# First weight units of the next block split before the meeting point, into tiles that are dead by then, and a third gate pair of layer one issued earlier

## The chip, the cores and the metric

The kernel runs on one core of a Trainium2 chip. Five engines take part, each with its own instruction queue: TensorE (PE; its weight loads are shown as PEld), VectorE (DVE), ScalarE (ACT), GpSimd (POOL) and SyncE (SP), which issues the DMAs. The metric is the device time of one execution in microseconds. Before the change the median of three runs is 835.58 us.

## The reference

The program computes a two-layer encoder on 256 tokens of width 1024 in float32. Each layer has a token mixer and a feed-forward network (FFN), each inside two normalisations:

```python
h = rmsnorm(x, g_mix_pre[l])
z = h @ w_in[l] + b_in[l]
y_m = mlstm_branch(...) @ w_up_mlstm[l]          # 4 heads of 128, both directions
y_f = fourier_branch(...) @ w_up_fourier[l]
y_s = s5_branch(...)                             # ends in a gated product with w_glu
gates = sigmoid(z[..., OFF_GATE:])               # three gates of width 1024
mixed = gates[0]*y_m + gates[1]*y_f + gates[2]*y_s
x = x + rmsnorm(mixed @ w_out[l], g_mix_post[l])
h = rmsnorm(x, g_ffn_pre[l])
f = square(relu(h @ w_ffn1[l])) @ w_ffn2[l]      # d_ff = 4096
x = x + rmsnorm(f, g_ffn_post[l])
```

So there are four blocks in a row (mixer 0, FFN 0, mixer 1, FFN 1), and the step from a block to the next is always the same: a sum over the whole width, a normalisation, the residual, another normalisation, and then the first product of the next block.

## The kernel before

**Weights.** All weights arrive in float32 and are multiplied in three products (high by high, high by low, low by high). A unit of weights is a tile of 128 x 1024 elements. `wload` makes one in three steps: a DMA on SP's queue into a `raw` tile (L200), ScalarE rounds it to the high part `whi` (L202), VectorE subtracts to get the low part `wlo` (L204). The `raw` tiles come from a ring of five, `whi` and `wlo` from rings of four; some units go to two larger rings, `ringA` and `ringB`, which other data use too. A slot of `raw` is free when `wlo` is done, one of `whi` and `wlo` when the last matmul of that unit is.

**Two forms of product.** In the body of a block the weights are the stationary operand and the tokens stream, 256 columns at a time (`mm3`, L262 to L264). At the start of a block the tokens are normalised one half (t=0, 128 tokens) after the other (t=1), and the first output columns are computed with the tokens stationary and the weights streaming, 512, 272 or 256 columns at a time (`tokens`, L278 to L281). In `tokens`, `hhi` and `hlo` are the high and low parts of the transposed normalised tokens, shown as `hT`. For t=0 the products with the low parts of the weights are put last (L295), for t=1 they stand beside the others.

**The meet.** Between two blocks `meet` puts together four strands: the last products of the old block for t=0 (`products(0)`) and t=1 (`products(1)`, "P"), the chains of normalisation for t=0 ("0") and t=1 ("1"), and the first units of the next block's weights, a `Feed` with the rounding of a unit ("h") and its subtraction ("l"). A chain runs through: two squares on ScalarE (L378), a small power on GpSimd (L340, L342), the gain and the residual on VectorE (L380, L386), two squares again (L355), GpSimd again, the second gain on VectorE (L361), eight transposes on TensorE (L188), and the high and low part of the result on ScalarE and VectorE (L370, L371). The string `MEET` gives the order of these steps on ScalarE and VectorE; the order on TensorE, and of what has no letter in the string, comes from a scheduler. Meet 0 is between mixer 0 and FFN 0, meet 1 between FFN 0 and mixer 1 (between the layers), meet 2 between mixer 1 and FFN 1.

**The Feed.** For an FFN it holds six units: four of 512 columns and two of 256. For layer 1's mixer it holds three units of the gates' projection of 272 columns (`igf`) and four of the values' projection `v`, 512 columns. `meet` empties it.

**The end of a mixer.** After the Fourier part, gates and products alternate: the mLSTM heads are normalised (L964), transposed and gated (L974) into `ym` (high part L976 on ScalarE, low part L977 on VectorE, both in `ringB`). `glu_up` multiplies the S5 result with `w_glu`, `own_gate` computes a gate for 256 output columns, and `mlstm_up` multiplies `ym` with `w_up_mlstm` and adds the gated parts. Two of the four own gates are issued before `glu_up`, two inside `mlstm_up`.

## Time and profile before

| | |
|---|---|
| median of three runs | 835.58 us (835.45 to 836.53) |
| the profiled execution | 834.29 us, of which the span from first to last instruction is 831.6 us |
| granted TensorE clock, mean | 0.998 of full speed |
| TensorE busy | 810.7 us of 831.6 (97%), 5825 matmuls |
| VectorE busy | 597.6 us (72%) |
| ScalarE busy | 472.4 us (57%) |
| GpSimd busy | 30.3 us (4%) |

The durations in a timeline are those of single instructions. Matmuls overlap each other, so for TensorE the distance from one start to the next is what an instruction costs, not its duration. "x8" joins eight instructions in a row, and the number in brackets is the idle time of the engine just before, with the instruction that ended it. Idle time of an engine other than TensorE costs nothing by itself.

### The profile page before, as it was taken

To read this page: it belongs to the slowest core of one execution; us is meant where nothing else is said; L and a number is where in the kernel's file an instruction comes from. 1 tells how busy PE (TensorE), PEld (TensorE's weight loads), DVE (VectorE), ACT (ScalarE), POOL (GpSimd) and SP (SyncE) were. 2 spreads that over 40 slices of the span, in tenths; PEclk is the share of its full clock that TensorE was granted. 3 is DMA by queue.
4 is the path that set the end of the run, shared out by engine and by line. 5 is a ranking of instruction groups with operands and counts; after the bars stand their busy time and mean duration, and the time that the engine had idled before them with its cause. 6 is when DMAs were issued, how large, how long until landed. Compare 5 with 4: busy or idle time off the path is not lost.

```text
span 831.6 us, 14910 instructions
## 1 busy us (share of the span) xinstructions
PE 810.7 (97%) x5825; PEld 749.4 (90%) x5825; DVE 597.6 (72%) x1071; ACT 472.4 (57%) x784; POOL 30.3 (4%) x51
## 2 busy tenths in 40 slices
PE   7999999998999999999999999999999999999996
PEld 5899999998878999999879999999997899999995
DVE  5898899887685567667568798776876755555563
ACT  4668764586464458467654355666865444444451
POOL 1000200000020000000010010000000100000000
PEclk9999999999999999999999999999999999999999
DMA  8785843554755564765837554555666555566651
GB/s 264 222 229 142 247 121 103 152 177 148 257 138 179 185 188 137 235 186 186 271 96 229 152 179 128 152 178 153 176 185 215 181 158 193 185 186 195 181 174 50
DMA packets 122262, 147.87 MB, mean 178 GB/s; under 512 B 22310, under 2 KB 104398, under 8 KB 121936
## 3 DMA queue, kind: packets, MB, share of 16 engines
q1 hardware_dynamic: 122044, 146.66, 57.9%
q8 instruction: 45, 0.74, 0.4%
q10 hardware_dynamic: 148, 0.27, 0.1%
q14 instruction: 25, 0.20, 0.1%
HBM read 144.33 MB, written 2.57 MB: 177 GB/s over the span
## 4 chain that ended last, share of the span: by engine, by line
PE 71%; DVE 2%; ACT 1%; issue 1%; POOL 1%; DVEq 0%; POOLq 0%; ACTq 0%
PE mm L262 12%; PE mm L264 12%; PE mm L263 12%; PE acc L263 8%; PE acc L264 8%; PE acc L262 8%; PE mm L279 2%; PE mm L278 2%; PE mm L295 1%; PE mm L188 1%; PE mm L281 1%; PE acc L743 1%; PE acc L939 1%; DVE wlo L204 1%; DVE x_sb L386 0%
## 5 line engine op out<-in xcount | busy, mean ns | idle before, releaser
L204 DVE TENSOR_TENSOR wlo<-raw,whi 128x1024 fp32r<-128x1024 f32 (+1 forms) x237 | 287.6, 1215 | 153.1 <-ACT whi L202 152.1
L202 ACT ACTIVATE whi<-raw 128x1024 fp32r<-128x1024 f32 (+1 forms) x237 | 248.5, 1052 | 241.3 <-PE mm L263 141.6
L262 PE MATMUL mm<-hT,whi 128*128 128x256 f32 x1024 | 290.9, 284 | 0.0
L264 PE MATMUL mm<-hT,wlo 128*128 128x256 f32 x1024 | 290.4, 284 | 0.0
L263 PE MATMUL mm<-hT,whi 128*128 128x256 f32 x1024 | 290.2, 283 | 0.0
L262 PEld LDWEIGHTS mm<-hT,whi 128*128 128x128 f32 x1024 | 192.8, 188 | 1.5
L263 PEld LDWEIGHTS mm<-hT,whi 128*128 128x128 f32 x1024 | 192.9, 188 | 1.1
L264 PEld LDWEIGHTS mm<-hT,wlo 128*128 128x128 f32 x1024 | 193.3, 189 | 0.2
L263 PE MATMUL acc<-wlo,ringB 128*128 128x512 f32 x280 | 109.3, 392 | 0.7 <-DVE wlo L204 0.7
L264 PE MATMUL acc<-whi,ringB 128*128 128x512 f32 x280 | 108.8, 391 | 0.0
L262 PE MATMUL acc<-whi,ringB 128*128 128x512 f32 x280 | 106.2, 390 | 0.0
L263 PEld LDWEIGHTS acc<-wlo,ringB 128*128 128x128 f32 x280 | 52.6, 188 | 12.1 <-DVE wlo L204 1.9
L264 PEld LDWEIGHTS acc<-whi,ringB 128*128 128x128 f32 x280 | 52.6, 188 | 11.0
L262 PEld LDWEIGHTS acc<-whi,ringB 128*128 128x128 f32 x280 | 52.6, 188 | 10.2
L279 PE MATMUL mm<-whi,hT 128*128 128x512 f32 (+1 forms) x84 | 30.3, 369 | 1.9 <-DVE hT L371 1.8
L906 DVE SCALAR_TENSOR_TENSOR t1k<-ringB,pc,t1k 128x254 f32<-128x254 f32 (+1 forms) x64 | 31.0, 484 | 0.9
L278 PE MATMUL mm<-whi,hT 128*128 128x512 f32 (+1 forms) x84 | 30.5, 373 | 0.7 <-ACT whi L202 0.5
L262 PE MATMUL mm<-ringB,whi 128*128 128x256 f32 x96 | 27.4, 286 | 1.7 <-ACT ringB L976 1.7
L380 DVE SCALAR_TENSOR_TENSOR w2k<-acc,ringA 128x512 f32<-128x512 f32 x16 | 10.6, 688 | 24.7 <-ACT t1k L378 24.7
L263 PE MATMUL mm<-ringB,whi 128*128 128x256 f32 x96 | 27.3, 285 | 0.0
L264 PE MATMUL mm<-ringB,wlo 128*128 128x256 f32 x96 | 27.2, 284 | 0.0
L378 ACT ACTIVATE t1k<-acc 128x512 bf16<-128x512 f32 x16 | 9.5, 595 | 30.4 <-PE acc L264 30.4
(334 smaller groups left out, 1156.8 us busy)
## 6 DMA issues: line engine op xcount, KB each, us to landing
raw<-in_w_ffn_dram SPq DMA_DIRECT2D x128, 512.0 KB
raw<-in_w_in_dram SPq DMA_DIRECT2D x84, 512.0 KB
raw<-in_w_out_dram SPq DMA_DIRECT2D x16, 512.0 KB
raw<-in_w_glu_dram SPq DMA_DIRECT2D x16, 256.0 KB
raw<-in_w_up_mlstm_dram SPq DMA_DIRECT2D x8, 512.0 KB
ringB<-md SPq DMA_DIRECT2D x2, 1024.0 KB
raw<-in_w_up_fourier_dram SPq DMA_DIRECT2D x4, 512.0 KB
raw<-in_w_in_dram SPq DMA_DIRECT2D x4, 408.0 KB
```

What stands on the lines that cost most here:

```text
L188: nc.tensor.transpose(o, i, cst[:k, C_ID:C_ID + k])
L202: act(hi, raw, AF.Copy)
L204: latest[0] = V.tensor_sub(lo, raw, hi.bitcast(F32)).ins
L262: mm(o, lhi, rhi, start=start, stop=False)
L263: mm(o, lhi, rlo, start=False, stop=False)
L264: mm(o, llo, rhi, start=False, stop=stop)
L278: mm(o, hhi[:, k, tt], hi, start=k == 0, stop=False)
L279: mm(o, hlo[:, k, tt], hi, start=False, stop=False)
L281: mm(o, hhi[:, k, tt], lo, start=False, stop=k == NK - 1)
L378: act(junk(), ps[c], AF.Square, accum_out=ss[:, c:c + 1])
L380: stt(f, ps[c], ROOT_D, gpost[:, half(c)], ALU.mult, ALU.mult)
L906: stt(u[:, lo_:hi_], z[:, lo_ + o:hi_ + o], col(l, "cw", j * 8 + i), u[:, lo_:hi_], ALU.mult, ALU.add)
```

## The change

Five things are changed together.

- The ring of `raw` tiles has four slots in place of five. The room goes to a small tile `pre`; the S5 tables `QT` and `Wt` become two tiles each for every layer, and `yg`, `oth` and `gx` are tiles that can be taken again under the same name once they are dead.
- `Feed` units get places: an FFN's four units of 512 columns go to `QT0`, `QT1`, `Wt0`, `Wt1`, the first of 256 columns to `tabC` and `tabS`, the last to the ring of `whi`. Layer 1's first two `igf` units go to `oth` with `yg` and to `gx` with `pre`.
- These units are split before the meet: after the second and fourth step of `glu_up` and after the first three of `mlstm_up` for the FFN's, in the FFN's steps 12 and 14 for layer 1's `igf`. The strings of `MEET` become shorter accordingly, and both layers use the same one.
- `tokens` issues four high products, then (for t=1) four with the low weights, then four with `hlo`, where it alternated one by one.
- In layer 0 three own gates are issued before `glu_up`, not two.

The diff, cut to its core:

```diff
-MEET = (("l0h0lh0l0Pl1hh1ll11ll", "hl0h0hlh0l0hPl1h1llll11l"), "hl0h0llP0101h11")
+MEET = ("0000Phl1111", "00P0hl0h1l1h1h1")
-    wp = ctx.enter_context(tc.tile_pool(name="wp", bufs=5))
+    wp = ctx.enter_context(tc.tile_pool(name="wp", bufs=4))
...
         raw = wp.tile(shape, F32, tag="raw", name=nm("raw"))
-        if in_ring:
+        if isinstance(in_ring, tuple):
+            if len(in_ring) == 1:
+                both = per([P, 2] + shape[1:], in_ring[0], F32R)
+                hi, lo = both[:, 0], both[:, 1]
+            else:
+                hi, lo = (per(shape, tag, F32R) for tag in in_ring)
+        elif in_ring:
...
-    def tokens(t, parts, together):
+    def tokens(t, parts, together, step=NK // 2):
...
-            for k in range(NK):
-                hi, lo = (w[:, k % kn, :] for w in units[k // kn])
-                mm(o, hhi[:, k, tt], hi, start=k == 0, stop=False)
-                mm(o, hlo[:, k, tt], hi, start=False, stop=False)
+            def part(a, i, ks, last=False):
+                for k in ks:
+                    mm(o, a[:, k, tt], units[k // kn][i][:, k % kn, :], start=k == 0 and a is hhi and i == 0,
+                       stop=last and k == NK - 1)
+
+            for k0 in range(0, NK, step):
+                ks = range(k0, min(k0 + step, NK))
+                part(hhi, 0, ks)
                 if t > 0:
-                    mm(o, hhi[:, k, tt], lo, start=False, stop=k == NK - 1)
+                    part(hhi, 1, ks)
+                part(hlo, 0, ks, t > 0)
...
-        return Feed([(iu, pieces_of(w, k0, min(3, NK - k0), OFF_IG, NIGF)) for k0 in (0, 3, 6)] +
+        spare = [None] * 3 if l == 0 else [("oth", "yg"), ("gx", "pre"), None]
+        return Feed([(iu, (*pieces_of(w, k0, min(3, NK - k0), OFF_IG, NIGF), spare[k0 // 3])) for k0 in (0, 3, 6)] +
...
                 stt(pair(th1, n2), z1, 0.5, pair(th1, n2), ALU.mult, ALU.add)
+                if n2 % 2:
+                    after.lo()
                 tick(B)
...
                 put_mix(mix, n2, th0)
+                if n2 < 3:
+                    after.lo()
 
         fourier_up()
-        gates = [own_gate(n2) for n2 in range(2)]
+        gates = [own_gate(n2) for n2 in range(3 if l == 0 else 2)]
...
-    GROUPS = ((512, None), (256, "A"))
+    GROUPS = ((512, [("QT0",), ("QT1",), ("Wt0",), ("Wt1",)]), (256, [("tabC", "tabS"), None]))
...
             f1(c)
+            if c >= NF // 2 - 4 and c % 2 == 0:
+                after.lo()
```

Where this moves instructions shows at two meets. The first place is ScalarE's queue in meet 1, from the steps that follow the transposes of t=0 (before: around them) to the second `v` unit, here `ringA_5088`. `acc` L378 and `x_sb` L355 are the two pairs of squares of t=1. Before:

```order
L378 ACTIVATE t1k_5050,ss_5049<-acc_3257 128x512
L378 ACTIVATE t1k_5054,ss_5049<-acc_3258 128x512
L370 ACTIVATE hT_84<-acc_5062 128x4x128
L370 ACTIVATE hT_84<-acc_5069 128x4x128
L355 ACTIVATE t1k_5079,ss_5078<-x_sb 128x512
L355 ACTIVATE t1k_5081,ss_5078<-x_sb 128x512
L202 ACTIVATE whi_5004<-raw_5003 128x1024
L370 ACTIVATE hT_84<-acc_5095 128x4x128
L370 ACTIVATE hT_84<-acc_5102 128x4x128
L202 ACTIVATE ringA_5088<-raw_5087 128x1024
```

The same place after the change, where L394, L371 and L386 are the former L378, L355 and L370, and `ringA_5069` is the second `v` unit:

```order
L386 ACTIVATE hT_5_84<-acc_5054 128x4x128
L386 ACTIVATE hT_5_84<-acc_5061 128x4x128
L213 ACTIVATE whi_4922<-raw_4921 128x1024
L394 ACTIVATE t1k_5073,ss_5072<-acc_3255 128x512
L394 ACTIVATE t1k_5077,ss_5072<-acc_3256 128x512
L371 ACTIVATE t1k_5089,ss_5088<-x_sb_78 128x512
L371 ACTIVATE t1k_5091,ss_5088<-x_sb_78 128x512
L213 ACTIVATE ringA_5069<-raw_5068 128x1024
L213 ACTIVATE ringA_5098<-raw_5097 128x1024
L213 ACTIVATE whi_5242<-raw_5241 128x1024
```

The squares of the sum (L394) have moved behind the high parts of t=0 and behind the first `v` unit `whi_4922`; the second `v` unit follows the squares of t=1 in both, and directly so now.

TensorE's queue at the same meet, before, from the last products of `igf` for t=0 to the transposes of t=1 (`acc_5095`, `acc_5102`); `mm_5155` are the values of t=0:

```order
L295 MATMUL mm_5129<-wlo_4969,hT_84 128x272 x3
L295 MATMUL mm_5129<-wlo_4988,hT_84 128x272 x2
L278 MATMUL mm_5155<-whi_5004,hT_84 128x512
L279 MATMUL mm_5155<-whi_5004,hT_85 128x512
L278 MATMUL mm_5155<-whi_5004,hT_84 128x512
L279 MATMUL mm_5155<-whi_5004,hT_85 128x512
L188 MATMUL acc_5095<-cst,w2k_5091 128x128 x4
L188 MATMUL acc_5102<-cst,w2k_5093 128x128 x4
```

After the change, with `mm_5162` as the values of t=0 and `acc_5109`, `acc_5116` as the transposes of t=1:

```order
L311 MATMUL mm_5136<-wlo_4801,hT_5_84 128x272 x2
L289 MATMUL mm_5162<-whi_4922,hT_5_84 128x512 x2
L289 MATMUL mm_5162<-ringA_5069,hT_5_84 128x512 x2
L289 MATMUL mm_5162<-whi_4922,hT_6_85 128x512 x2
L289 MATMUL mm_5162<-ringA_5069,hT_6_85 128x512 x2
L192 MATMUL acc_5109<-cst_79,w2k_5101 128x128 x4
L289 MATMUL mm_5162<-ringA_5098,hT_5_84 128x512 x2
L192 MATMUL acc_5116<-cst_79,w2k_5103 128x128 x4
```

Products with the second `v` unit, `ringA_5069`, stand now ahead of the transposes of t=1, and one pair with the third unit between them; before, only the first unit did.

The second place is VectorE's queue in meet 0, the chain of t=1 from its first gain (before L380) to its second (before L361). Before:

```order
L380 SCALAR_TENSOR_TENSOR w2k_3070<-acc_2902,ringA_2893 128x512
L380 SCALAR_TENSOR_TENSOR w2k_3074<-acc_2903,ringA_2893 128x512
L386 SCALAR_TENSOR_TENSOR x_sb<-w2k_3070,rs_480_3078,x_sb 128x512
L386 SCALAR_TENSOR_TENSOR x_sb<-w2k_3074,rs_480_3078,x_sb 128x512
L204 TENSOR_TENSOR ringA_3063<-raw_3062,ringA_3063 128x1024
L204 TENSOR_TENSOR ringA_3081<-raw_3080,ringA_3081 128x1024
L361 SCALAR_TENSOR_TENSOR w2k_3098<-x_sb,rs_487_3094,ringA_2893 128x512
L361 SCALAR_TENSOR_TENSOR w2k_3100<-x_sb,rs_487_3094,ringA_2893 128x512
```

After the change, where L396, L402, L215 and L377 are the former L380, L386, L204 and L361; the units 3260, 3290 and 3327 are later weights of the FFN, and ScalarE's queue has their three roundings between the two pairs of squares of t=1, where it had two of `ringA`:

```order
L396 SCALAR_TENSOR_TENSOR w2k_3075<-acc_2928,ringA_2923 128x512
L396 SCALAR_TENSOR_TENSOR w2k_3079<-acc_2929,ringA_2923 128x512
L402 SCALAR_TENSOR_TENSOR x_sb_78<-w2k_3075,rs_498_3083,x_sb_78 128x512
L215 TENSOR_TENSOR wlo_3260<-raw_3258,whi_3259 128x1024
L402 SCALAR_TENSOR_TENSOR x_sb_78<-w2k_3079,rs_498_3083,x_sb_78 128x512
L215 TENSOR_TENSOR wlo_3290<-raw_3288,whi_3289 128x1024
L215 TENSOR_TENSOR wlo_3327<-raw_3325,whi_3326 128x1024
L377 SCALAR_TENSOR_TENSOR w2k_3096<-x_sb_78,rs_503_3094,ringA_2923 128x512
L377 SCALAR_TENSOR_TENSOR w2k_3098<-x_sb_78,rs_503_3094,ringA_2923 128x512
```

One subtraction has moved between the two residual sums of t=1, and two stand ahead of the second gain, where two stood before.

## Rows read from the trace of the kernel before

**Rows 1.** Page, section 1: busy us, share of the span, instructions.

```profile
PE 810.7 (97%) x5825; PEld 749.4 (90%) x5825; DVE 597.6 (72%) x1071; ACT 472.4 (57%) x784; POOL 30.3 (4%) x51
```

**Rows 2.** Busy us (instructions) per engine in stretches of 10 us, then clock, DMA share, GB/s.

```profile
590.00:600.00 10.00, 10.00 (x86) 10.00 (x85) 10.00 (x15) 7.27 (x15) 0.00 (x0) 1.00 0.71 204
630.00:640.00 10.00, 9.12 (x41) 7.21 (x39) 4.59 (x7) 5.60 (x11) 1.87 (x4) 1.00 0.49 158
```

**Rows 3.** Timeline of TensorE, first meet: start us, duration, instruction [wait <- releaser].

```profile
234.17 1.32 PE L188 MATMUL acc<-cst,w2k 128*128 128x128 f32 x8 [1.02 <-DVE w2k L361]
...
236.56 0.50 PE L279 MATMUL mm<-whi,hT 128*128 128x512 f32 x1 [0.56 <-DVE hT L371]
...
244.90 1.10 PE L188 MATMUL acc<-cst,w2k 128*128 128x128 f32 x8
...
253.39 0.50 PE L263 MATMUL acc<-wlo,ringB 128*128 128x512 f32 x1 [0.36 <-DVE wlo L204]
```

**Rows 4.** Timeline of TensorE, meet between the layers.

```profile
420.34 0.39 PE L264 MATMUL acc<-whi,ringB 128*128 128x512 f32 x1
...
425.78 0.39 PE L264 MATMUL acc<-ringA,ringB 128*128 128x512 f32 x1
426.72 1.32 PE L188 MATMUL acc<-cst,w2k 128*128 128x128 f32 x8 [0.56 <-DVE w2k L361]
...
429.18 0.39 PE L279 MATMUL mm<-whi,hT 128*128 128x272 f32 x1 [0.72 <-DVE hT L371]
...
432.80 0.50 PE L278 MATMUL mm<-whi,hT 128*128 128x512 f32 x1 [0.49 <-ACT whi L202]
...
433.84 1.16 PE L188 MATMUL acc<-cst,w2k 128*128 128x128 f32 x8
```

**Rows 5.** Timeline of TensorE, end of layer 0's mixer.

```profile
190.07 0.60 PE L188 MATMUL acc<-cst,hm 128*128 128x128 f32 x4
191.30 0.79 PE L188 MATMUL acc<-cst,hm 128*128 128x128 f32 x4 [0.63 <-DVE t1k L974]
193.83 0.39 PE L262 MATMUL mm<-ringB,whi 128*128 128x256 f32 x1 [1.74 <-ACT ringB L976]
```

**Rows 6.** Timeline of ScalarE, meet between the layers.

```profile
427.41 1.26 ACT L370 ACTIVATE hT<-acc 128x512 fp32r<-128x512 f32 x2 [0.52 <-PE acc L188]
...
431.08 0.63 ACT L355 ACTIVATE t1k<-x_sb 128x512 bf16<-128x512 f32 x1
...
431.71 1.04 ACT L202 ACTIVATE whi<-raw 128x1024 fp32r<-128x1024 f32 x1
```

**Rows 7.** Timeline of VectorE, meet between the layers.

```profile
429.64 1.41 DVE L386 SCALAR_TENSOR_TENSOR x_sb<-w2k,rs,x_sb 128x512 f32<-128x512 f32 x2
432.88 1.41 DVE L361 SCALAR_TENSOR_TENSOR w2k<-x_sb,rs,ringA 128x512 f32<-128x512 f32 x2 [1.83 <-POOL rs L342]
```

**Rows 8.** Timeline of ScalarE, first meet.

```profile
238.10 2.01 ACT L202 ACTIVATE ringA<-raw 128x1024 fp32r<-128x1024 f32 x2
```

**Rows 9.** Timeline of VectorE, first meet.

```profile
240.76 2.35 DVE L204 TENSOR_TENSOR ringA<-raw,ringA 128x1024 fp32r<-128x1024 f32 x2
243.88 1.41 DVE L361 SCALAR_TENSOR_TENSOR w2k<-x_sb,rs,ringA 128x512 f32<-128x512 f32 x2 [0.76 <-POOL rs L342]
```

**Rows 10.** Timeline of GpSimd, first meet.

```profile
238.32 0.30 POOL L340 TENSOR_SCALAR rs<-ss 128x1 f32<-128x1 f32 x1 [4.99 <-ACT t1k L378]
...
241.70 1.50 POOL L340 TENSOR_SCALAR rs<-ss 128x1 f32<-128x1 f32 x1 [2.44 <-ACT t1k L355]
```

**Rows 11.** Timeline of ScalarE, end of layer 0's mixer.

```profile
192.56 0.81 ACT L1062 ACTIVATE w2k<-mm,pch 128x256 f32<-128x256 f32 x2
193.28 1.70 ACT L976 ACTIVATE ringB<-t1k,pch 128x256 fp32r<-128x256 f32 x4
```

**Rows 12.** Timeline of VectorE, end of layer 0's mixer.

```profile
192.69 1.23 DVE L204 TENSOR_TENSOR wlo<-raw,whi 128x1024 fp32r<-128x1024 f32 x1
193.83 1.67 DVE L977 SCALAR_TENSOR_TENSOR ringB<-t1k,pch,ringB 128x256 fp32r<-128x256 f32 x4
```

More of the change, by code (lines that the diff above doesn't have):

```diff
@@ L154, in small, with per @@
         return sp.tile(shape, F32, tag=tag, name=nm(tag), bufs=bufs)
-    def per(shape, name, dt=F32):
-        return cp.tile(shape, dt, tag=name, name=name)
+    def per(shape, tag, dt=F32):
+        return cp.tile(shape, dt, tag=tag, name=nm(tag))
     act = nc.scalar.activation
@@ L176, in encoder_kernel, with new_tables @@
     G.memset(v_sb[:, :, :, DH:DH + 1], 1.0)
-    QT = per([P, 2, 2 * NGP, P], "QT")
-    Wt = per([P, 2, 2 * NGP, LT, 32], "Wt")
-    Tt = per([P, NGP, P], "Tt")
-    tabC = per([P, 2 * NGP, JN], "tabC")
-    tabS = per([P, 2 * NGP, JN], "tabS")
+    tabs = {}
+    def new_tables(l):
+        tabs[l] = ([per([P, 2 * NGP, P], f"QT{r}") for r in range(2)],
+                   [per([P, 2 * NGP, LT, 32], f"Wt{r}") for r in range(2)],
+                   per([P, NGP, P], "Tt"), per([P, 2 * NGP, JN], "tabC"), per([P, 2 * NGP, JN], "tabS"))
+        return tabs[l]
     C_F, C_RHO, C_TURN, C_AF, C_A = 0, 2, 3, 4, 6
@@ L571, in s5_tables @@
         W16 = 2 * NGP
+        QT, Wt, Tt, tabC, tabS = tabs[l] if l in tabs else new_tables(l)
         tb_ps = (lambda: acc_ps(1)) if l == 0 else mm_ps
@@ L863, in stabilisers @@
         act(em, em, AF.Exp)
-        Gx = [sp.tile([P, NH, P], F32, tag="gx", name=nm("gx"), bufs=2) for _ in range(2)]
+        gx = per([P, 2, NH, P], "gx")
+        Gx = [gx[:, d] for d in range(2)]
         for d in range(2):
@@ L980, in encoder_kernel @@
     qk_scale = 0.25 * DH ** -0.5
-    yg = [per([P, 2, S], f"yg{i}", F32R) for i in range(2)]
-    oth = per([P, NH, S], "oth")
     def mixer_units(l, iu, vu):
@@ L996, in mixer @@
         spent[:] = 0.0, 0.0
+        yg_ = per([P, 2, 2, S], "yg", F32R)
+        yg = [yg_[:, i] for i in range(2)]
+        oth = per([P, NH, S], "oth")
         wm, wf, wg = a["w_up_mlstm"][l], a["w_up_fourier"][l], a["w_glu"][l]
@@ L1021, in mixer @@
                 ((0, [p_igf, p_v]), (1, [p_igf, p_v])):
-            tokens(t, parts, False)
+            tokens(t, parts, False, 1 if l == 0 else NK // 2)
         if l == 0:
@@ L1180, in mixer @@
         gpre = [gg[:, 0, half(c)] for c in range(2)]
-        meet(products, norms(0, aps[0], gg[:, 1], gpre), norms(1, aps[1], gg[:, 1], gpre), after, MEET[0][l])
-    GROUPS = ((512, None), (256, "A"))
+        meet(products, norms(0, aps[0], gg[:, 1], gpre), norms(1, aps[1], gg[:, 1], gpre), after, MEET[0])
+    GROUPS = ((512, [("QT0",), ("QT1",), ("Wt0",), ("Wt1",)]), (256, [("tabC", "tabS"), None]))
     def ffn_units(l, groups):
@@ L1192, in ffn_units @@
             groups.append((f0, n, kn, []))
-            specs += [(groups[-1][3], (*pieces_of(a["w_ffn1"][l], k0, kn, f0, n), where)) for k0 in range(0, NK, kn)]
+            specs += [(groups[-1][3], (*pieces_of(a["w_ffn1"][l], k0, kn, f0, n), where[k0 // kn]))
+                      for k0 in range(0, NK, kn)]
             f0 += n
```

24 lines of the change are left out of this document (13 added, 11 removed).

## Prediction

> **What bounds the kernel now.** I read the page first: TensorE is busy for 97% of the span [rows 1], so the time is its matmuls, which the change leaves at the same number and shapes, plus about 21 us in which it stands idle (831.6 less 810.7). Next the table of stretches of 10 us: some 2 us of the 21 lie in each of four stretches, the end of layer 0's mixer and the three meets, and the rest at the start and the tail, which the change leaves alone. The last meet shows 9.12 busy of 10 us [rows 2]. Then the timeline of TensorE in these stretches, where the reader is to see the bracketed waits and what ended them.
>
> - Meet 0: 1.02 us before the transposes of t=0 (released by L361 on VectorE), 0.56 us for the low part of the tokens (L371), none before the transposes of t=1 at 244.90, and 0.36 us for a late `wlo` [rows 3]. Meet 2 has the same order and shows the same waits.
> - Meet 1: 0.56 us before the transposes of t=0, 0.72 for the low part, 0.49 for a late `whi`; the transposes of t=1 follow at 433.84 without a wait [rows 4].
> - End of layer 0's mixer: 0.63 and 1.74 us for `ym` [rows 5].
>
> So at most 1.94 us can be saved in each of meets 0 and 2, 1.77 in meet 1 and 2.37 at `ym`: 8.0 us in all. In each meet the chain of t=1 was just hidden. Whether it still is decides.
>
> **Meet 1.** I count from X, the start of t=0's transposes (426.72 before). Before X, TensorE works on what is left behind t=0's last matmul, which started at 420.34. The 24 starts from there to 425.78 [rows 4] give 0.227 us each. After the change 20 matmuls are left there, so 4 x 0.227 = 0.9 us of cover is gone. The chain of t=0 loses two interleaved splits, for which I count 0.1, as it waits mostly for its own squares and GpSimd. Cost: 0.8 us.
>
> Behind X the queues shown in the section on the change decide. ScalarE: the high parts of t=0 end at X + 1.95 (427.41 + 1.26), `whi_4922` takes 1.04 [rows 6] to X + 3.0, two squares of about 0.6 to X + 4.2. From a last square to VectorE's next step it takes 1.17 us (431.08 + 0.63 to 432.88 [rows 6, 7]), so to X + 5.4. VectorE: the subtraction of that unit (about 1.2, half of the 2.35 for two) ends after the first gains at about X + 6.1, the residual sums take 1.41 [rows 7] to X + 7.5. The second pair of squares then ends at X + 8.1 (0.63 for the last [rows 6]), and only behind it stands the rounding of the second `v` unit, 1.0 us: ready at X + 9.1. TensorE arrives there much earlier. Transposes 1.32, 24 matmuls of 272 columns at 0.13 (23 took from 429.18 to 432.80 less the wait of 0.49 [rows 4]), a short wait of 0.2 for the low part and two matmuls of the first `v` unit at 0.23 make X + 5.1. It waits some 4.1 us, then runs six matmuls (1.4 us) and reaches the transposes of t=1 at X + 10.6, where before it needed 433.84 - 426.72 = 7.1. Four matmuls (0.9 us) more are done by then, so 2.6 us are lost. With the 0.8 above, meet 1 costs 3.4 us, though its three old waits become smaller or vanish. Bounds: if the squares of the sum come early and VectorE's subtraction is not in the way, the wait is 2 us shorter (1.2 in all); if a raw tile lands late as well, 1 us longer (4.4).
>
> **Meets 0 and 2.** Here the old block leaves 21 matmuls behind t=0's last, before 22: 0.23 us later for everything that follows X. The wait of 0.56 goes, since eight high products (1.4 us) come ahead of the first low one; the 48 matmuls of t=0's tokens take 8.5 us (47 of them ran from 236.56 to 244.90 [rows 3]) and end at X + 9.8. But the chain of t=1 is no earlier. Its squares end as before at about X + 3.9 (238.10 less 234.17 [rows 8]). Then three roundings instead of two, 3.0 us against 2.01, hold ScalarE to X + 6.95. VectorE's first residual sum, 1.17 us after the squares and 0.7 long, ends at X + 5.9, the moved-in subtraction of 1.2 at X + 7.2 (its rounding ends at X + 4.9), the second sum at X + 7.9, the last square at X + 8.55. Now GpSimd and VectorE meet. Before, L340 took 1.50 us instead of 0.30 [rows 10] and ended at 243.20, just as VectorE's two subtractions ended (240.76 + 2.35 = 243.11 [rows 9]). After, the two subtractions run from X + 7.9 to X + 10.3. If GpSimd is held until both are done, as the row shows, the second gain starts 0.7 later (243.20 to 243.88 [rows 9, 10]), at X + 11.0, and the transposes follow its first half at X + 11.8, against 10.73 before (244.90 less 234.17): 1.1 us later, plus the 0.23. The 0.36 for the late `wlo` is saved, and 0.1 at the low part of t=1. Sum: 0.85 us lost per meet, 1.7 for both.
>
> The Trainium skill (SBUF — State Buffer, section "Who interferes with whom") says that a VectorE instruction with two SBUF inputs and a GpSimd instruction that reads SBUF hold a shared port for one whole instruction, and that whoever starts first has it. By that rule GpSimd, which began at 241.70 during the first subtraction, would have had its turn when that one ended at about 241.95; the row shows it held past the second too, to 243.20. By the rule a meet would cost 0.05 us instead of 0.85 (the second rival below). The row decides.
>
> Bounds for each of the two: -1.2 if the chain of t=1 is hidden (the transposes at the end of the tokens, 0.93 earlier, and 0.46 behind, with the 0.23 to pay), and +1.6 if a raw tile is late in ScalarE's queue.
>
> **The end of layer 0's mixer.** T is the start of the transposes (190.07 before). Both sides of the chain keep their order: ScalarE's normalisation of the heads stands behind a rounding that waits for a slot, and a rounding and the gate's tanh stand ahead of the first `ym`; the first matmul with `ym` came at T + 3.76 [rows 5], with the rounding, 0.81 of tanh and the first of four high parts [rows 11] in that time. After the change the same operations stand there with tanh first, so T + 3.8, and the 2.37 us stay. What changes is the work behind: before, gate matmuls followed at once and hid the low parts of `ym`, which VectorE made behind a subtraction of 1.23 us [rows 12]. After, the third gate is already done, four matmuls (0.5 us) follow, and the next needs a low part, ready at about T + 5.0: the rounding and so the subtraction begin 0.8 later than the 192.69 of before, behind the tanh, end at 194.7, and the first low part takes 0.4. TensorE stands there at T + 4.3. Cost: 0.7 us. Bounds: -2.4 if the whole wait went with the earlier gate, +1.5.
>
> **What is hidden.** The same number of units is split, only earlier. Their loads move with them on SP's queue, ahead of weights that are used sooner. At the end of layer 1's mixer VectorE is full from 590 to 600 us [rows 2] and gets two or three subtractions of 1.2 us more; the stretches beside it have room, and rings of four hold that much ahead, so I count nothing. Without that cover it costs up to 2 us. Of the four `raw` slots the feed holds one before meet 0, and `igf` and `v` hold two at the end of FFN 0, where the others must turn over for the last four units. The DMA engines are busy for 0.71 and 0.49 of the two stretches [rows 2], not the limit by themselves: nothing, bound 2 us. The start and the tail keep their waits.
>
> **The sum.** 3.4 + 1.7 + 0.7 = 5.8 us. On the profiled execution, 834.29 us (the span and 2.7 us around it), that gives 840.1; this execution is 1.29 us below the median of the runs, so on the median's scale I forecast 841.4 us.
>
> **The rivals.**
>
> - *Fewer splits in the meets free both chains* (faster). Each meet has one unit of its feed left to split where it had most of them. If the chain of t=1 is thereby done before the tokens of t=0, all waits behind X go: 1.2 in each of meets 0 and 2, 1.2 in meet 1 with 0.8 to pay, and `ym` gains its 2.4 when the earlier gate gives the heads time. Together 2.4 + 0.4 + 2.4 = 5.2: 830.4. It decides in meet 1, on whether the second `v` unit is rounded by X + 5.0; the order on ScalarE puts it behind four squares, which speaks against it. For it: three of the named waits do lose their cause.
> - *The gains pay for the late chain* (no change). If GpSimd gets its turn between the two subtractions, the second gain starts behind the second of them, at X + 10.3, and the transposes at X + 11.0: 0.27 + 0.23 - 0.46 = 0.05 per meet. With meet 1 at its lower bound of 1.2 and `ym` even, 836.9 results. The 1.50 us of L340 speak against it. (The Trainium skill's section named above is this rule.)
> - *Starved splits* (slower still). Two raw slots in FFN 0 and a full VectorE in layer 1's mixer cost their 2 us each on top of the 5.8: 845.4. For it: VectorE's full stretch; against it: in the trace no `tokens` or `mm3` row inside a block waits for a split.
>
> **How the numbers follow.** Chances: forecast 0.52, freed chains 0.20, even 0.14, starved 0.14. The range must reach from the upper part of the freed case to the lower part of the starved one: 833.5 to 844.5; the forecast's own range, meet 1 between 1.2 and 4.4 and the other meets between 0 and 1.3 each, is 837.5 to 843.3. A difference of 0.2% is 1.7 us, about what a measurement of this kernel can tell from none. Faster by more than that takes the freed case and little else: 0.21. The even case and the near edge of the forecast: 0.13. Slower: 0.66.
>
> **What would show it.** In the profile after: a wait of some 4 us of TensorE near 432 us, at a `tokens` matmul (L289), released by ScalarE's rounding into `ringA`; a wait of 1 to 2 us at the transposes of t=1 (L192) in meets 0 and 2, released by L377, with the L356 of GpSimd beside it at over 1 us; about 1.5 us before t=0's transposes in meet 1; no wait on `hT` from L387 over 0.3 us; and a wait on `ringB` at L273 near 193 us as before, with a second one at L274. It is wrong if the transposes of t=1 come without a wait, above all in meet 1, or if new waits on `whi` or `wlo` (L213, L215) appear inside a block.

## The result and the profile after

The changed kernel takes 845.13 us (median of 4 runs, 843.56 to 848.03), the kernel before 835.52 on the same chip (834.78 to 836.53): a ratio of 1.011, 95% interval 1.0081 to 1.014. Slower, as forecast, but by 9.6 us where 5.8 were forecast, and 0.6 us beyond the upper end of the range. The profiled execution took 843.64 us with a span of 841.9.

TensorE's busy time and its number of matmuls are those of before [rows 1]; that the busy time is the same is chance, since a lower clock added to it and a shorter step of the matmuls took from it, as the rows below show:

```profile
PE 810.8 (96%) x5825; PEld 748.3 (89%) x5825; DVE 596.9 (71%) x1071; ACT 471.2 (56%) x784; POOL 29.1 (3%) x51
```

TensorE's waits after the change (us in total, times, longest). The first two rows are the meets (1.0 of the 8.4 is the start of the kernel), L1244 is the transposes of the FFN's first results, at the end of meets 0 and 2, and the rest is the mixers' ends:

```profile
PE acc L192 <- DVE w2k L377: 8.4, 8, 1.7
...
PE mm L289 <- ACT ringA L213: 3.7, 1, 3.7
PE mm L273 <- ACT w2k L1141: 3.1, 2, 2.3
PE acc L192 <- DVE t1k L994: 1.4, 1, 1.4
PE mm L273 <- ACT ringB L996: 1.2, 1, 1.2
PE mm L192 <- DVE w2k L1244: 1.0, 2, 0.5
PE mm L274 <- DVE ringB L997: 0.5, 1, 0.5
```

To find what a wait list misses, take for each matmul how much later it started after the one before than its shape's steady step (118 ns for 256 columns, 227 for 512), and add these up by stretch, in the two profiled executions:

| stretch (us) | before | after | more | forecast |
|---|---|---|---|---|
| 180-220, end of layer 0's mixer | 3.4 | 10.0 | 6.7 | 0.7 |
| 220-280, meet 0 | 4.3 | 5.4 | 1.1 | 0.85 |
| 420-460, meet 1 | 4.5 | 8.6 | 4.1 | 3.4 |
| 580-620, end of layer 1's mixer | 0.5 | 2.2 | 1.7 | 0 |
| 620-700, meet 2 | 4.4 | 5.6 | 1.2 | 0.85 |
| all the rest | 22.4 | 17.9 | -4.5 | 0 |
| sum | 39.4 | 49.7 | 10.3 | 5.8 |

So three things want an explanation: 6.0 us more than forecast in layer 0's mixer, about 3 more in the other stretches, and 4.5 us that came back where nothing waited.

**The meets.** TensorE in meet 0, where [rows 3] are before, and in meet 1, where [rows 4] are:

```profile
239.51 1.32 PE L192 MATMUL acc<-cst,w2k 128*128 128x128 f32 x8 [1.22 <-DVE w2k L377]
251.25 1.32 PE L192 MATMUL acc<-cst,w2k 128*128 128x128 f32 x8 [1.71 <-DVE w2k L377]
...
433.33 1.32 PE L192 MATMUL acc<-cst,w2k 128*128 128x128 f32 x8 [1.51 <-DVE w2k L377]
438.01 0.63 PE L289 MATMUL mm<-whi,hT 128*128 128x512 f32 x2
442.34 0.91 PE L289 MATMUL mm<-ringA,hT 128*128 128x512 f32 x2 [3.69 <-ACT ringA L213]
```

In meet 0 the transposes of t=1 stand at X + 11.74 (251.25 less 239.51); the forecast said X + 11.8. Meet 2 has the same distance (662.07 less 650.33). In meet 1 the second `v` unit is used at X + 9.01; forecast, X + 9.1. Its wait was put at 4.1 and is 3.69. ScalarE's queue shows the reason, the rounding behind both squares of t=1:

```profile
440.62 0.63 ACT L371 ACTIVATE t1k<-x_sb 128x512 bf16<-128x512 f32 x1
...
441.24 1.99 ACT L213 ACTIVATE ringA<-raw 128x1024 fp32r<-128x1024 f32 x2
```

In meet 0, GpSimd and VectorE met as in [rows 9, 10], GpSimd's row first:

```profile
248.18 1.58 POOL L356 TENSOR_SCALAR rs<-ss 128x1 f32<-128x1 f32 x1 [3.58 <-ACT t1k L371]
```

```profile
247.25 2.35 DVE L215 TENSOR_TENSOR wlo<-raw,whi 128x1024 fp32r<-128x1024 f32 x2
250.44 1.41 DVE L377 SCALAR_TENSOR_TENSOR w2k<-x_sb,rs,ringA 128x512 f32<-128x512 f32 x2 [0.84 <-POOL rs L358]
```

GpSimd began during the first of two subtractions (247.25 to 248.4) and ended 0.16 us after the second (249.60): held past both, and meet 2 shows 1.58 again. The rival that let it in between (the Trainium skill, SBUF — State Buffer, section "Who interferes with whom", by which the instruction that began first has the port for one instruction) is not what this row shows.

**The end of layer 0's mixer.** TensorE, where [rows 5] are before, and then ScalarE:

```profile
186.90 0.28 PE L275 MATMUL mm<-yg,wlo 128*128 128x256 f32 x1
189.43 0.39 PE L273 MATMUL mm<-yg,whi 128*128 128x256 f32 x1 [2.25 <-ACT w2k L1141]
...
190.96 0.41 PE L273 MATMUL mm<-yg,whi 128*128 128x256 f32 x1
191.17 0.41 PE L274 MATMUL mm<-yg,whi 128*128 128x256 f32 x1
...
193.67 0.28 PE L274 MATMUL mm<-hT,whi 128*128 128x256 f32 x1
193.79 0.28 PE L275 MATMUL mm<-hT,wlo 128*128 128x256 f32 x1
...
200.54 0.74 PE L192 MATMUL acc<-cst,hm 128*128 128x128 f32 x4 [1.35 <-DVE t1k L994]
202.46 0.73 PE L273 MATMUL mm<-ringB,whi 128*128 128x256 f32 x4 [1.18 <-ACT ringB L996]
203.71 0.55 PE L274 MATMUL mm<-ringB,whi 128*128 128x256 f32 x1 [0.52 <-DVE ringB L997]
```

```profile
182.67 0.89 ACT L1138 ACTIVATE w2k<-mm,pch 128x256 f32<-128x256 f32 x2
186.13 1.06 ACT L213 ACTIVATE Wt<-raw 128x1024 fp32r<-128x1024 f32 x1 [2.58 <-DMA raw<-in_w_ffn_dram]
187.10 1.04 ACT L213 ACTIVATE whi<-raw 128x1024 fp32r<-128x1024 f32 x1
188.04 0.45 ACT L1141 ACTIVATE w2k<-mm,pc 128x256 f32<-128x256 f32 x1
```

The early rounding for the next block (`Wt<-raw`) stands in ScalarE's queue ahead of the read-out of `glu_up`'s sums (L1141), which it has nothing to do with. Its load was issued only at 181.05 (a row of SP's queue):

```profile
181.05 0.37 SPq L211 DMA_DIRECT2D raw<-in_w_ffn_dram  x1
```

So ScalarE stands still for 2.58 us, and TensorE, with no free sum to write to, for 2.25. The `ym` waits stay beside it (1.35, 1.18 and 0.52; 2.37 in all before): waits alone, 2.9 us more. Layer 1's mixer has such rows too: ScalarE stood still for 2.76 us before a `Wt<-raw` at 591.19, and TensorE for 0.80 us before L1141 had read a sum out, at 599.43; that the one brought the other there is not shown.

**The clock.** The other half is in the rows at 190.96 and 193.67: the step between two matmuls is 0.21 us and then 0.12. Stretches after (PE, PEld, DVE, ACT, POOL busy, then granted clock, DMA share, GB/s):

```profile
190.50:193.50 3.00, 3.00 (x16) 3.00 (x15) 3.00 (x9) 2.55 (x5) 0.42 (x1) 0.50 0.86 285
...
204.00:208.00 4.00, 4.00 (x23) 4.00 (x23) 0.85 (x3) 0.00 (x0) 0.00 (x0) 0.60 0.39 135
208.00:212.00 4.00, 4.00 (x35) 4.00 (x35) 1.90 (x3) 1.55 (x2) 0.00 (x0) 1.00 0.00 0
444.00:448.00 4.00, 4.00 (x23) 3.46 (x22) 2.60 (x5) 2.02 (x4) 0.00 (x0) 0.73 0.25 57
```

A clock of 0.50 is 1.2 GHz in place of 2.4: 16 matmuls in 3 us. After the change the granted clock drops three times for some 3.4 us, 0.4 to 1.3 us after TensorE resumed: behind the 2.25, behind the `ym` waits and behind the 3.69 of meet 1. Each drop costs half of its length, 1.7 us, so 5.1 us in all. The profiled execution of before has a clock of 1.00 in these stretches; other executions of it, with a lower mean clock, do not run as fast (e1).

### The profile page after: what moved, and what is told of

Same layout as the page of the kernel before. It is cut to its first block, busy times and chain, and to the rows that moved or that the text cites. A ratio compares the mean times of both kernels' runs of the same rounds, so it can differ in the third digit from the quotient of the medians.

```text
span 841.9 us, 14893 instructions
## 1 busy us (share of the span) xinstructions
PE 810.8 (96%) x5825; PEld 748.3 (89%) x5825; DVE 596.9 (71%) x1071; ACT 471.2 (56%) x784; POOL 29.1 (3%) x51
## 4 chain that ended last, share of the span: by engine, by line
PE 62%; issue 24%; ACT 5%; DMA 4%; DVE 3%; POOL 1%; SPq 0%; DVEq 0%; POOLq 0%; ACTq 0%
PE mm L274 12%; PE mm L273 12%; PE mm L275 12%; PE acc L273 5%; PE acc L274 5%; PE acc L275 5%; PE mm L289 4%; DMA raw<-in_w_ffn_dram 3%; PE acc L762 2%; ACT whi L213 1%; PE acc L192 1%; DVE wlo L215 1%; PE acc L798 1%; PE acc L959 1%; PE acc L801 1%
## 5 line engine op out<-in xcount | busy, mean ns | idle before, releaser
L215 DVE TENSOR_TENSOR wlo<-raw,whi 128x1024 fp32r<-128x1024 f32 (+1 forms) x229 | 277.7, 1216 | 134.9 <-ACT whi L213 133.2
L213 ACT ACTIVATE whi<-raw 128x1024 fp32r<-128x1024 f32 (+1 forms) x229 | 240.4, 1054 | 224.0 <-PE mm L274 128.2
L274 PE MATMUL mm<-hT,whi 128*128 128x256 f32 x1024 | 289.2, 282 | 0.0
L274 PEld LDWEIGHTS mm<-hT,whi 128*128 128x128 f32 x1024 | 193.3, 189 | 1.1
L274 PE MATMUL acc<-wlo,ringB 128*128 128x512 f32 x280 | 108.4, 390 | 0.0
L274 PEld LDWEIGHTS acc<-wlo,ringB 128*128 128x128 f32 x280 | 52.6, 188 | 10.2 <-DVE wlo L215 0.3
L274 PE MATMUL mm<-ringB,whi 128*128 128x256 f32 x96 | 28.0, 293 | 0.5 <-DVE ringB L997 0.5
L289 PE MATMUL mm<-whi,hT 128*128 128x272 f32 (+2 forms) x112 | 26.1, 346 | 0.0
L396 DVE SCALAR_TENSOR_TENSOR w2k<-acc,ringA 128x512 f32<-128x512 f32 x16 | 10.4, 686 | 20.5 <-ACT t1k L394 20.5
L356 POOL TENSOR_SCALAR rs<-ss 128x1 f32<-128x1 f32 x16 | 7.4, 460 | 484.3 <-ACT t1k L394 289.5
L394 ACT ACTIVATE t1k<-acc 128x512 bf16<-128x512 f32 x16 | 9.4, 593 | 23.1 <-PE acc L275 23.1
```

The source lines that it names most:

```text
L213: act(hi, raw, AF.Copy)
L215: latest[0] = V.tensor_sub(lo, raw, hi.bitcast(F32)).ins
L274: mm(o, lhi, rlo, start=False, stop=False)
L289: mm(o, a[:, k, tt], units[k // kn][i][:, k % kn, :], start=k == 0 and a is hhi and i == 0, stop=last and k == NK - 1)
L394: act(junk(), ps[c], AF.Square, accum_out=ss[:, c:c + 1])
L396: stt(f, ps[c], ROOT_D, gpost[:, half(c)], ALU.mult, ALU.mult)
```

## Experiments

The time of the kernel before, measured beside the experiments below, is 835.8 to 837.5 (medians of 7 to 23 runs), and each ratio is to it. Where in memory a kernel's tiles start matters from e13 on; e1, e3, e4 and e7 to e11 have the places of the changed kernel, e2, e5, e6 and e12 those of before.

**e1: no wait, does the clock stay?** Sixteen unused matmuls in the long wait of meet 1.

```diff
+                    if t == 0 and not together and kn == 2 and step > 1 and k == 1 and a is hhi and i == 0:
+                        extra = mm_ps()
+                        for _ in range(16):
+                            mm(extra, hhi[:, 0, tt], units[0][0][:, 0, :], start=True, stop=True)
```

> The changed kernel with 16 extra matmuls of 512 columns put where TensorE waits 3.7 us in the meet between the layers, ahead of the products with the second v unit; their result is not used. Theory A (the wait costs itself and then about 1.7 us more, since the granted clock falls to 0.50 for some 3.4 us behind it): the 16 matmuls (3.6 us) fill the wait, the clock behind it stays 1.00, and the span falls by 1.7 us against the changed kernel (841.9 to about 840.2), though work was added. Theory B (the lower clock has another cause, such as the time since the block began): clock and span stay as they are, 841.9.

844.15 us (ratio 1.0089, 1.0069 to 1.011). In meet 1 the clock held:

```profile
440.00:444.00 4.00, 4.00 (x18) 2.91 (x17) 2.16 (x5) 3.96 (x7) 0.87 (x2) 1.00 0.71 236
444.00:448.00 4.00, 4.00 (x28) 3.57 (x27) 3.97 (x7) 2.41 (x4) 0.00 (x0) 1.00 0.33 95
660.00:670.00 10.00, 9.93 (x42) 8.04 (x43) 3.87 (x8) 2.27 (x5) 0.00 (x0) 0.83 0.23 82
```

23 matmuls in 444 to 448 became 28. All four traces that keep a wait of 3.7 us there (the changed kernel, e8, e9 and e18) have a drop beside it; e1 and e2, without the wait, have none: in meet 1 the drop goes with the wait. The total hardly fell, since this execution has another drop in meet 2, behind the same 1.71 us wait that had none in the changed kernel. So drops differ from run to run, and the length of a wait does not settle them: 3.48 us in e2's `glu_up` had none behind it. This is also how runs of one kernel spread: by mean clock, executions of before lie at 833 to 835 us for 0.998 and at 836.5 to 838.8 for 0.992.

**e2 and e3: one half of the change taken back.** e2 puts the meet between the layers back, e3 the early splits of the mixers and the meets behind them.

```diff
 e2
-MEET = ("0000Phl1111", "00P0hl0h1l1h1h1")
+MEET = ("0000Phl1111", "hl0h0llP0101h11")
-            if c >= NF // 2 - 4 and c % 2 == 0:
-                after.lo()
 e3
+MEET = (("l0h0lh0l0Pl1hh1ll11ll", "hl0h0hlh0l0hPl1h1llll11l"), "00P0hl0h1l1h1h1")
-                if n2 % 2:
-                    after.lo()
-                if n2 < 3:
-                    after.lo()
+    GROUPS = ((512, [None] * 4), (256, ["A", "A"]))
```

> The changed kernel with the meet between the layers put back: no igf split inside the FFN, old order string there. Theory A (the time went to the new order of that meet, 3.0 us of waits and 1.7 us of lower clock): 4.7 us less than the changed kernel, about 840.4. Theory B (the time went to raw tiles, of which there are four now instead of five): nearly nothing, since the ring keeps four slots: 844 or more.

> The changed kernel with the meets from mixer to FFN put back: the six FFN units are split in the meet again, in the rings of before, with the old order strings. Theory A (the early splits hold ScalarE's queue: 2.4 us of wait and 1.7 of lower clock in layer 0's glu_up, 1.4 in each of the two meets, 1.3 at the end of layer 1's mixer): about 8 us less than the changed kernel, 837. Theory B (four raw slots): the wait in glu_up goes, as no feed unit holds a slot there, but the meets keep new waits: about 841.

e2: 846.44 (1.0124, 1.0093 to 1.0155). Meet 1 is as before, with no drop, but layer 0's wait grew to 3.48 us, behind a ScalarE that waited 5.0 us for one load, and two drops came elsewhere: the wait on a load is not the same in each program. Read as it stands, the time speaks for theory B. But without the early `igf` split the tile `pre` (3,264 bytes) is gone, so the weights' tiles stand where they do before, and the matmuls have the longer step of before (rows at e13). Beside e18, the changed kernel at those places, e2 is 4.4 us faster (1.0124 against 1.0177), near the 4.7 of theory A, though the two intervals overlap. e3: 831.70 (0.9944, 0.9924 to 0.9965), 13.4 us below the changed kernel. The end of layer 0's mixer has one wait left, and the clock there is 1.00. The rows are TensorE there and in meet 1, then stretches:

```profile
190.60 0.41 PE L192 MATMUL acc<-cst,hm 128*128 128x128 f32 x2 [0.27 <-DVE t1k L994]
...
425.11 1.32 PE L192 MATMUL acc<-cst,w2k 128*128 128x128 f32 x8 [1.49 <-DVE w2k L377]
...
434.12 0.73 PE L289 MATMUL mm<-ringA,hT 128*128 128x512 f32 x2 [2.35 <-ACT ringA L213]
```

```profile
180.00:200.00 20.00, 19.73 (x170) 19.53 (x170) 18.53 (x30) 17.93 (x39) 1.85 (x2) 1.00 0.43 140
...
426.90:430.20 3.30, 3.30 (x16) 3.23 (x15) 2.47 (x5) 2.26 (x6) 0.86 (x2) 0.50 0.49 159
...
434.20:440.00 5.80, 5.80 (x35) 5.07 (x36) 5.77 (x9) 3.90 (x5) 0.00 (x0) 1.00 0.44 141
```

So the waits in the mixers come with the early splits, and without them the third gate does remove the `ym` waits. e3 also takes back the places of the units and the order of meets 0 and 2; e10 below keeps the places. In meet 1 its drop stands behind the wait of 1.49 us, and none behind the longer one of 2.35.

**e4: two gates again.**

```diff
-        gates = [own_gate(n2) for n2 in range(3 if l == 0 else 2)]
+        gates = [own_gate(n2) for n2 in range(2)]
```

> The changed kernel with two own gates ahead of glu_up in layer 0, as before. Theory A (the third gate takes the cover from ym's low parts: 0.7 us, and the long wait at ym lets the clock fall: 1.7 us): about 2.4 us less than the changed kernel, 842.7, with the wait in glu_up unchanged. Theory B (the third gate gives the heads time, so without it ym's wait grows): 1 us more, 846.

848.32 (1.0151, 1.0112 to 1.0191), theory B's way, though the interval meets that of the changed kernel. The wait gathers in one place. VectorE's rows show the heads coming late: between their statistics (L970, L971), on which `hm` waits, stands an early subtraction for the FFN (`tabS<-raw,tabC`), beside work of the mixer itself:

```profile
199.48 3.17 PE L192 MATMUL acc<-cst,hm 128*128 128x128 f32 x8 [7.74 <-ACT hm L984]
```

```profile
192.23 0.48 DVE L970 BATCH_NORM_STATS2 bst<-hm 128x6 f32<-128x128 f32 x2
...
193.21 1.22 DVE L215 TENSOR_TENSOR tabS<-raw,tabC 128x1024 fp32r<-128x1024 f32 x1
...
196.09 0.24 DVE L971 BATCH_NORM_AGGREGATE mv<-bst 128x2 f32<-128x6 f32 x2
```

That one row is 1.22 us of the 7.74; with e3, where the wait is gone, the reading is that the splits delay the heads and that in the changed kernel the third gate hides a part of it.

**e8: a fifth `raw` slot, e9: no early split in `glu_up`** (the four of a mixer all in `mlstm_up`), in the changed kernel.

```diff
 e8
-    wp = ctx.enter_context(tc.tile_pool(name="wp", bufs=4))
+    wp = ctx.enter_context(tc.tile_pool(name="wp", bufs=5))
-    tp = ctx.enter_context(tc.tile_pool(name="tp", bufs=8))
+    tp = ctx.enter_context(tc.tile_pool(name="tp", bufs=7))
 e9
-                if n2 % 2:
-                    after.lo()
-                if n2 < 3:
-                    after.lo()
+                after.lo()
```

> The changed kernel with five raw slots as before (and seven instead of eight slots for a 1 KB scratch tile, which makes the room). Theory A (the early splits stand in ScalarE's queue ahead of what frees TensorE's banks in glu_up, whenever their tile lands): the wait in glu_up becomes shorter, since the tile of the fourth FFN unit is requested about 1 us earlier, but stays at 1 us or more; 842 to 845. Theory B (four slots starve the loads): the wait goes, and its lower clock: 840 or less.

> The changed kernel with four of the FFN's units split early, all inside mlstm_up, and none inside glu_up (two are left for the meet). Theory A (the two splits inside glu_up stand in ScalarE's queue ahead of the normalisation of the heads and wait there for their load, so the heads come late): layer 0's waits of 2.25 and of 1.35, 1.18 and 0.52 us go with the lower clock behind them; the meets keep theirs: 7 us less than the changed kernel, about 838. Theory B (any early split costs its time on ScalarE and VectorE there): half of it stays, 841 to 842.

e8: 843.44 (1.009, 1.0066 to 1.0115): ScalarE still waits 3.1 and 2.3 us for such loads, so a fifth slot does not remove them; why the loads come that late stays open. e9: 847.51 (1.0134, 1.0119 to 1.0149), a miss: layer 0's waits fell only from 5.3 to 3.4 us, and those of meets 0 and 2 rose (2.4 and 2.6 before t=0's transposes, 1.4 before the last). Moving the splits within the mixer moves the wait. How much of the loss is the waiting for loads and how much the work of the splits on the two engines, which its two theories were to tell apart, stays open.

**e5, e6, e12: the third gate, the new order of `tokens`, and both, in the kernel before.**

```diff
 e5, e12
+        gates = [own_gate(n2) for n2 in range(3 if l == 0 else 2)]
 e6, e12
+    def tokens(t, parts, together, step=NK // 2):
...
+            tokens(t, parts, False, 1 if l == 0 else NK // 2)
```

> The kernel before with one part of the change: three own gates ahead of glu_up in layer 0. Theory A (by the run without the early FFN splits, the third gate alone lets the heads be normalised inside glu_up, and ym's waits of 0.63 and 1.74 us go): 2.0 to 2.4 us less than the kernel before, ratio 0.9972. Theory B (the prediction: the order around ym stays, and 0.7 us of cover is lost): ratio 1.0008.

> The kernel before with one part of the change: tokens in blocks of four. Theory A (the waits for the low part, 0.56, 0.72 and 0.56 us, go, but the chain of t=1 was hidden by 0.3 us only, so most of it comes back as a wait at the transposes of t=1): 0.3 to 1.2 us less, ratio 0.999. Theory B (the waits are simply gone): 2.6 us less (0.83, 0.99 and 0.83 from start to start), ratio 0.997.

> The kernel before with tokens in blocks of four and three gates ahead of glu_up in layer 0, nothing else of the change. Theory A (the third gate saves ym's wait of 2.4 us, tokens in blocks gains nothing by itself): 833 to 834 on a chip where before takes 836, ratio 0.997. Theory B (what e3 and e7 gained comes from the early igf splits and the meet between the layers, not from these): ratio 1.000 or more.

e5: 834.81 (0.9991, 0.9974 to 1.0007). The `ym` waits are gone, but meet 0 gives it back, with a wait of 2.38 where 1.02 stood [rows 3] and a drop behind it:

```profile
232.86 1.61 PE L188 MATMUL acc<-cst,w2k 128*128 128x128 f32 x8 [2.38 <-DVE w2k L361]
```

e6: 838.28 (1.0021, 1.0006 to 1.0037), slower than either theory: the waits on `hT` go, new ones on `whi` (0.73) and `wlo` (0.53) come. e12: 835.50 (0.9994, 0.9983 to 1.0004). No gain, though e3, with these, the new meet between the layers and four `raw` slots, was 5.75 us faster than the kernel before, measured beside it; this is what stayed open until e13.

**e7, e10, e11: from e3 on.** e7 gives meet 1 another order; e10 adds the dead places to e7 without early splits; e11 has t=1's squares ahead of t=0's transposes as well.

```diff
 e7, against e3
-"00P0hl0h1l1h1h1"
+"00P01hl01h1l1"
 e10 and e11, against e7
-    GROUPS = ((512, [None] * 4), (256, ["A", "A"]))
+    GROUPS = ((512, [("QT0",), ("QT1",), ("Wt0",), ("Wt1",)]), (256, [("tabC", "tabS"), None]))
 e11
-MEET = (("l0h0lh0l0Pl1hh1ll11ll", "hl0h0hlh0l0hPl1h1llll11l"), "00P01hl01h1l1")
+MEET = (("hl0h0lhl0P1l01hl11hlhl", "hl0h0lhl0P1l01hl11hlhl"), "00P01hl01h1l1")
```

> The kernel of the run without the early FFN splits (831.7 us), with another order in the meet between the layers: the squares of t=1's sum right behind those of t=0, the first v unit behind the squares of t=1's tokens, and the second v unit behind all. Theory A (the 2.35 us wait for the second v unit and the 1.7 us of lower clock behind it come from the order of ScalarE's queue): no such wait, at most 1.5 us at the transposes of t=1 instead, clock 1.00 there; 2 to 3 us less, 829. Theory B (the wait comes from the load of that unit): it stays, 831.7.

> The kernel of e7 (829.8 us; no early FFN split, other order between the layers), with the FFN's units put into the dead tiles all the same, split in the meet in the order of before. Theory A (f2's first weights wait in meets 0 and 2, 0.73 and 0.53 us, because the feed holds the slots of whi and wlo): these waits go, the chain of t=1 gets a third split ahead of it and is 1 us later: 0.5 us less per meet, 828.8. Theory B (they wait for their loads): 830 or more.

> The kernel of e10 with the squares of t=1's sum ahead of the transposes of t=0 in ScalarE's queue, and the FFN's last units behind the chain of t=1. Theory A (the order of the two in-order queues sets the meets): the chain of t=1 is ready by the end of t=0's first tokens, the waits at t=1's transposes stay under 0.5 us, and f2's waits go: 1 us less per meet than e7, about 827.8. Theory B (the chain's own length sets them): as e10.

e7: 829.77 (0.9928, 0.9908 to 0.9948): with the transposes of t=1 and its products with `igf` ahead of the second `v` unit, the 2.35 is gone, and 1.50, 0.83 and 0.25 remain in meet 1, with a drop behind the 1.50. By the medians it is 1.9 us faster than e3, but the two intervals overlap. e10: 834.66 (0.9986, 0.9972 to 1.0001) and e11: 841.21 (1.0056, 1.0039 to 1.0074), both misses: with the units split all at once in the meet, t=1 is late again (meet 0 of e10: 1.58 and 1.17 us before transposes; of e11: 1.92 before transposes, 0.97 and 1.17 before products). e10 has the same units at the same places as the changed kernel, without the early splits, and is 10.5 us faster, of which the order of meet 1 may account for 1.9: most of the loss goes with splitting early. The places of the units by themselves cost 4.9 us against e7, in the meets.

**e13 to e18: the places of the tiles.** The 4.5 us that came back lie in stretches without waits. There, each matmul of 256 columns simply follows sooner. A piece of the last FFN block, 48 such matmuls from the first row to the second, in the kernel before, the changed kernel, e14 and e2:

```profile
701.74 0.28 PE L262 MATMUL mm<-hT,whi 128*128 128x256 f32 x1
...
707.50 0.39 PE L262 MATMUL acc<-whi,ringB 128*128 128x512 f32 x1
```

```profile
701.70 0.28 PE L273 MATMUL mm<-hT,whi 128*128 128x256 f32 x1
...
707.40 0.40 PE L273 MATMUL acc<-whi,ringB 128*128 128x512 f32 x1
```

```profile
710.43 0.28 PE L263 MATMUL mm<-hT,whi 128*128 128x256 f32 x1
...
716.03 0.39 PE L263 MATMUL acc<-whi,ringB 128*128 128x512 f32 x1
```

```profile
718.05 0.28 PE L273 MATMUL mm<-hT,whi 128*128 128x256 f32 x1
...
723.82 0.39 PE L273 MATMUL acc<-whi,ringB 128*128 128x512 f32 x1
```

5.76, 5.70, 5.60 and 5.77 us: 120.0, 118.8, 116.7 and 120.2 ns each. The rows name no addresses, but the built programs do: the weights' tiles and the rings start at 480 modulo 512 bytes before (and in e2) and at 160 after, since the new tiles moved them, while `hT` stayed. So e13 to e18 only shift them, by an unused tile (192, 64, 320, 352, 384 and 320 bytes):

```diff
     par = per([P, C_A + 2 * (LT - 1), 32], "par")
+    G.memset(per([P, 48], "pad"), 0.0)
```

> The kernel before, with an unused tile of 192 bytes a partition allocated behind `par`, so that everything allocated behind it (raw, whi, wlo, the rings) starts 192 bytes later; hT keeps its place. The place of whi modulo 512 bytes is then 160, as in the changed kernel, where it is 480 in the kernel before. In the stretch 680 to 800 us (the last FFN block, no waits), the 256-column matmuls start 120.05 ns apart in the trace of before and 118.77 ns in the traces of the changed kernel and of e3; the 512-column ones 228.6 and 227.4. Theory A: the place of the weights' tiles sets this step; then 118.8 and 227.4 ns here, some 3,000 x 1.28 ns + 850 x 1.1 ns = 4.8 us less: about 831 us against 835.8. Theory B: the step differs for another reason (the new order of code, the pools); then 120.0 ns and the time of before.

> The same with a tile of 64 bytes: whi at 32 modulo 512, 32 modulo 128 (as in the changed kernel), 32 modulo 256 (160 there). Theory A with a period of 128 bytes or less: 118.8 ns and about 831 us. Theory A with a longer period: between 118.8 and 120 ns or another value. Theory B: 120.0 ns and the time of before.

> The version of e7 (829.77 us), with an unused tile of 320 bytes at the same place, so that whi stands at 480 modulo 512, as in the kernel before. Theory A: the matmuls of 256 columns in the last FFN block go back to 120.0 ns and the time rises by some 4.8 us to 834.5. Theory B: 118.8 ns and 829.8 us.

> The version of e7 with a tile of 352 bytes: whi and the rings start at a multiple of 512 bytes. Theory A: a step of its own for this place, at best below 118.8 ns (each 1 ns is some 3 us), else between 118.8 and 120; 827 to 834 us. Theory B: 118.8 ns and 829.8 us.

> The version of e7 with an unused tile of 384 bytes, so that whi and the rings start at 32 modulo 512, as in e14, where the 256-column matmuls of the last FFN block start 116.72 ns apart (117.85 in e16, 118.77 in e7). Theory A (the place alone sets the step): 116.7 ns here too, 1.13 x 3,000 = 3.4 us less than e16's 827.98, so about 824.6 us, level with e14 (825.05) or below it. Theory B (in e14 something else helps): 117.8 to 118.8 ns and 828 to 830 us.

> The changed kernel with an unused tile of 320 bytes, so that whi and the rings stand at 480 modulo 512, as in the kernel before: the change without the shift of places that came with it. Theory A: 120.0 ns between the matmuls of the last FFN block and about 4.5 us more than the 845.1 of the changed kernel, 849.6 us; what the change costs beside the places is then 14 us. Theory B: the cost of the change's waits is as it was and the places do nothing here: 845 us and 118.8 ns.

| place, modulo 512 | ns a matmul | code of before | code of e7 | changed code |
|---|---|---|---|---|
| 480 | 120.0 | 836.2 | 835.05 (e15) | 851.73 (e18) |
| 160 | 118.8 | 830.77 (e13) | 829.77 (e7) | 845.13 |
| 0 | 117.9 | | 827.98 (e16) | |
| 32 | 116.7 | 825.05 (e14) | 826.29 (e17) | |

Ratios to before: e13 0.9937 (0.9914 to 0.996), e14 0.9887 (0.9858 to 0.9916), e15 0.9993 (0.9977 to 1.0009), e16 0.9906 (0.9885 to 0.9927), e17 0.9883 (0.986 to 0.9907), e18 1.0177 (1.0147 to 1.0207). The step follows the place in every kernel, whichever its code: theory A. It also settles e12: at one place, e7's code and that of before are within 1.3 us of each other, so what looked like a gain of e3 and e7 was the shift of their tiles. And the changed code, at the place of before, costs 15.1 us (851.73 less 836.66, measured beside it; 12 to 17 by the interval). e17 has the least ratio and e14 the least median; the two intervals do not part them, and both beat both kernels. A shift of 64 bytes alone brings the kernel before to 825.05, some 11 us. Which of the shifted tiles it is, and why, was not tried.

## Why the prediction was wrong in size

- **Meets 1, 0 and 2 (3.4 and 1.7): the mechanism right, the sizes near.** The waits of meet 1 are 5.20 us against 1.77, 3.4 more; by the table it lost 4.1, of which 1.7 are the clock drop, so 2.4 without it. Meets 0 and 2 have the late t=1 to within 0.1 us of the place named and lost 1.1 and 1.2 where 0.85 was forecast. GpSimd was held for 1.58, as the row of before had shown. Not foreseen: 0.5 us before the transposes of L1244. (One slip: 3.4 less 2 is 1.4, not the 1.2 of meet 1's lower bound; it moves the forecast's own range by 0.2.)
- **The end of layer 0's mixer (0.7): the step that failed.** The prediction kept "the same operations" behind T and looked only there, to find a late low part of `ym` (0.52 at L274, where it was expected). The larger wait arose ahead of T, in `glu_up`. The stretch measured 6.7: 2.9 of waits, 3.4 of two clock drops and a small rest. That the waits behind T came out as forecast, 3.05 against 2.37 and so 0.7 more, is luck: the third gate alone takes the `ym` waits away (none in e5, 0.27 in e3), and they stayed because the early splits held the heads back. All the signs that the prediction named came, those in time some 10 us late, and most of the loss that it missed lay where none of them looked: in `glu_up` and in the clock.
- **"What is hidden. ... so I count nothing": the reason.** A split moved forward brings its own wait with it, for a load, onto an engine that works in order. The prediction named loads moved on SP's queue and looked for what they would hold up there; what stood behind the rounding on ScalarE, and behind the subtraction on VectorE, it asked for the meets only. e3 and e10, without these splits, are 13.4 and 10.5 us faster at the same places of the weights' tiles; e9 shows the wait moving with them. The bound of 2 us held for layer 1's mixer (1.7 measured), where TensorE waited for read-outs on ScalarE, not for the full VectorE.
- **No term for the clock.** Every wait was priced at its own length. In the profiled execution three drops cost another 1.7 us each; for the one in meet 1, e1 shows that it goes with the wait.
- **"TensorE's matmuls, which the change leaves at the same number and shapes": true, and not enough.** Their step changed by 1%, which hid about 5 us of a loss of 15 (e18). That the result lies only 0.6 us beyond the range is luck: what the step gave back is about what the three drops cost.
- **Rivals.** The even case did not come, and freed chains did not as a whole, though its earlier gate does free `ym` by itself (e5). Starved splits came near by its number (845.4), and splits that wait for their loads are its idea. But a fifth slot hardly changed the loss (e8), most of it lay in layer 0's mixer, which it had not named, and FFN 0 showed none of it; the number fits by luck, with drops and a shorter step in it that the rival did not have. (What was said against it overlooked a row: the one at 253.39 [rows 3] is an `mm3` row that waits 0.36 us for a `wlo`.)
